# Attention masks of a two-layer decoder kernel: masks kept in their own pool, one identity tile read with stride zero, and a first attention masked by GpSimd

## The chip, the cores and the metric

The kernel runs on one core of a Trainium2 chip. The metric is the device time of one launch in microseconds, from the first to the last instruction and what lies around them, as the median over several runs. TensorE does the matmuls (PE in the profile; PEld is its weight load), VectorE is DVE, ScalarE is ACT, GpSimd is POOL, and SyncE (SP) issues most of the transfers.

## The reference

Two layers run over 1024 prompt tokens and 32 sample tokens (8 sequences of 4). What matters here is layer 0:

- one projection gives the queries, keys and values of four attentions and a gate;
- attention A (g = 0 in the code) has 8 query heads on 2 key heads of size 64, a window of 128 keys back, and a learned sink in the denominator;
- attention B has three groups (g = 1, 2, 3) with windows and strides (128, 1), (512, 4), (2048, 16), 8 query heads on 2 key heads each, merged by their denominators;
- the sample tokens do the same attention against long caches of keys and values;
- then gate, output projection, residual and LayerNorm.

```
dist = query - key;  band = (dist >= 0) & (dist <= span)     # blocks of 128: own block and the one before
p = exp(where(band, q.k, -1e30) - max);  out = p @ v / sum(p)
x1 = LayerNorm(alpha * x + (mix * silu(z)) @ w_out)
```

Layer 1 (an mLSTM) comes after it and is not touched.

## The kernel before

The program is written as one stream of operations over tiles. The framework (`schedule_with_timeline_sim=True`) fixes each engine's order when the kernel is built: it walks a model of time and gives each engine, among the operations that are ready by the model, the one with the best priority. On the chip each engine and each queue of transfers keeps that order, so an operation that waits holds up all that stands behind it. Tiles come from pools that are laid out in SBUF as a stack; a new pool may cover the bytes of one that was released, and what is written there first waits for the last use of what lay there before.

Layer 0 goes in four steps.

1. `proj_kv` and `proj_q(0)` project the keys, the values and A's queries.
2. `projections()` (queries of B, in chunks `pj` of 384, 384 and 288 tokens, L199 to L201) is woven with `attention()`: A whole (`attn_a` for two key heads) and the row maxima of B's first two groups (`stats`, tile `st`).
3. `gate_path()` is woven with `attention_b()`: the last maxima, then `attn_b(0)` and the first nine blocks of `attn_b(1)`.
4. The pool `sm` is released (L967). The rest of `attn_b(1)` (`late`), the sample tokens' attention (`sample_attn`) and the first `merges` are woven. The sample attention loads its keys and values (inputs `in_kt`, `in_vc`) into tiles `KT` of a new pool `smt` with four buffers, 24 loads in all; their lines are L672 (scores `sS`) and L719 (outputs `so`). Then `out0` follows: the weights `in_wo` go through `wr` into `oh` and `ol`, `out_proj` multiplies them with the merged `M` into `py` (L165 to L167, 24 matmuls for each half of a block of 128 tokens, two PSUM banks for each half), and adds the residual `xr` (L870), which lies in a pool `lnp` opened above the weights.

`scores` makes a block of attention: for 128 queries of four heads and 128 keys it fills a PSUM tile `sc` with three matmuls of 512 columns, the first of which adds the mask: the weights are a 128x128 tile of `maskr`, the moving operand is four identities side by side, `ident4` (the trace writes it `ident`). Two Exp on ScalarE give `ph` (rounded) and `p`, VectorE or at times GpSimd takes `pl` = `p` - `ph`, and three matmuls of 512 columns add `ph` and `pl` times `V` to `av`. A has 15 blocks for each key head, 30 in all; B has 70. `maskr` and `ident4` lie in `sm`, at its start, followed by `sinkb`, `sinkc`, the two query tiles `QZ` and then the small ones (`ST`, `junk`, `NM`, `dn`, `nmc`). The last use of a small one is `finish(1, 0)` with `dn`, at the end of `attn_b(0)`.

GpSimd also makes the low part `wl` of each projection weight (L122) and a sum in the rotation (L215). ScalarE also takes `pj` out of PSUM (L112).

Of the kernel before, what the change touches and what calls it, by code (L numbers as in the profile page):

```python
# [4 lines left out]
F32 = mybir.dt.float32  # L5
F32R = mybir.dt.float32r
AF = mybir.ActivationFunctionType
# [46 lines left out]
def run(g):  # L54
    for _ in g:
        pass
# [41 lines left out]
class Builder:  # L98
# [351 lines left out]
    def scores(self, g, kv, hf, Q1, Q2, K1, K2, V, emit):  # L450
        nc = self.nc
        for qb in range(2 * hf, 2 * hf + 2):
            q0 = 128 * (qb % 2)
            bl = self.blocks(g, qb)
            sct, avt = self.bps
            av = self.pp.tile([66, 512], F32, tag=avt[qb % len(avt)], name="av")
            for bi, (kb, kind) in enumerate(bl):
                sc = self.pp.tile([128, 512], F32, tag=sct[self.nsc % len(sct)], name="sc")
                self.nsc += 1
                ks = slice(128 * kb, 128 * kb + 128)  # L460
                so = sc.rearrange("p (h q) -> p h q", h=4)
                mk = self.maskr[:, 256:384] if g == 3 else self.maskr[:, 128 - 128 * kind:256 - 128 * kind]
                nc.tensor.matmul(so, mk, self.ident4, start=True, stop=False)
                nc.tensor.matmul(so, K1[:, ks], Q1[:, :, q0:q0 + 128], start=False, stop=False)
                nc.tensor.matmul(so, K2[:, ks], Q2[:, :, q0:q0 + 128], start=False, stop=True)  # L465
                ph = self.ppool.tile([128, 512], F32R, tag="ph", name="ph")
                pl = self.ppool.tile([128, 512], F32R, tag="pl", name="pl")
                p = self.ppool.tile([128, 512], F32, tag="p", name="p", bufs=3)
                nc.scalar.activation(ph, sc, AF.Exp)  # L469
                nc.scalar.activation(p, sc, AF.Exp)  # L470
                if g and self.nsc % POOL_LO == 0:
                    nc.gpsimd.tensor_tensor(pl, p, f(ph), OP.subtract)
                else:
                    self.lo(pl, p, ph)
                first, last = bi == 0, bi == len(bl) - 1
                nc.tensor.matmul(av, V[:, kb, 64:130], ph, start=first, stop=False)
                nc.tensor.matmul(av[0:64], V[:, kb, 0:64], ph, start=False, stop=False, skip_group_check=True)
                nc.tensor.matmul(av, V[:, kb, 64:130], pl, start=False, stop=last)
            emit(qb, av)
            yield 1.1 * len(bl)  # L480
# [395 lines left out]
    def layer0(self):  # L876
        nc, tc, A, O = self.nc, self.tc, self.A, self.O
        dp = self.dram
        dt = lambda n, s: dp.tile(s, F32, name=n)

        self.QQ = [dt(f"QQ{g}", [129 * 8, TP]) for g in range(4)]
        self.QS = dt("QS", [4, 512, TS])

        self.KK, self.KS = dt("KK", [2 * 512, TP]), dt("KSd", [512, TS])

        self.VV = dt("VV", [TP, 8 * 128])
        self.NMB = [[dt(f"NMB{i}{g}", [4, TP]) for g in range(3)] for i in range(2)]

        self.OD = [[dt(f"OD{t}{i}", [65, 4, TP]) for i in range(2)] for t in range(2)]
        self.FD = [[dt(f"FD{t}{i}", [4, TP]) for i in range(2)] for t in range(2)]  # L890
        self.SZ = dt("SZ", [8, 128, T])
        self.KVN = dt("KVN", [TS, 2, 512])
        self.X1 = dt("X1", [T, 1024])

        self.X0 = [(self.xp.tile([128, 8, n], F32R, tag=f"xh{c}", name=f"xh{c}"),
                    self.xp.tile([128, 8, n], F32R, tag=f"xl{c}", name=f"xl{c}")) for c, (t0, n) in enumerate(CH)]
        self.wsp = tc.alloc_tile_pool(name="wsp", bufs=2, side="right")
        stage = self.stage = tc.alloc_tile_pool(name="stage", bufs=2, side="right")
        tmp = self.tmp = tc.alloc_tile_pool(name="tmp", bufs=1, side="right")
        self.proj_kv()  # L900
        with tc.tile_pool(name="qp", bufs=2) as self.qp, tc.tile_pool(name="kp", bufs=2) as self.kp, \
                tc.tile_pool(name="vp", bufs=2) as self.vp, tc.tile_pool(name="ppool", bufs=3) as self.ppool, \
                tc.tile_pool(name="odp", bufs=1) as self.odp:
            sm = self.sm = tc.alloc_tile_pool(name="sm", bufs=1)

            raw = self.wraw.tile([128, 1024], F32, tag="wraw", name="mkr")
            self.load(raw[:, 0:384], A['maskq'])
            self.maskr = self.sm.tile([128, 384], F32R, name="maskr")
            self.hi(self.maskr, raw[:, 0:384])
            self.maskq = f(self.maskr)  # L910
            self.ident4 = self.sm.tile([128, 4, 128], F32R, name="ident4")
            nc.vector.tensor_copy(self.ident4, self.ident.unsqueeze(1).to_broadcast([128, 4, 128]))
            self.sinkb = self.sm.tile([128, 64], F32, name="sinkb")
            self.load(self.sinkb, A['sinkb'])
            self.sinkc = self.sm.tile([32, 2], F32, name="sinkc")
            self.load(self.sinkc, A['sinkc'])
            self.QZ = [sm.tile([128, 4, 256], F32R, name=f"QZ{u}") for u in range(2)]
            for Q in self.QZ:
                nc.gpsimd.memset(f(Q[64:128]), 0.0)
            run(self.proj_q(0))  # L920
            self.done = 0
            self.bps = AB_PS[0]

            def projections():
                for g in (1, 2, 3):
                    yield from self.proj_q(g)
                    self.done = g

            def attention():
                for kv in range(2):  # L930
                    yield from self.attn_a(kv)
                for g in (1, 2):
                    while self.done < g:
                        yield None
                    for kv in range(2):
                        yield from self.attn_b_stats(g, kv)

            weave((projections(), W1[0]), (ahead(tc, attention(), AHEAD[0]), W1[1]))

            tmp.release()  # L940
            tmp = self.tmp = tc.alloc_tile_pool(name="tmpz", bufs=1, side="right")

            def gate_path():
                for j in range(8):
                    yield from self.proj_z0(j)

            def last(c):
                if c < 2:
                    self.merge0(1, 1, c, self.M, False)

            def attention_b():
                for kv in range(2):
                    yield from self.attn_b_stats(3, kv)
                    self.attn_b_max(kv)
                self.bps = AB_PS[1]
                yield from self.attn_b(0)
                late = self.late = self.attn_b(1, last)
                for _ in range(EARLY):
                    yield next(late)

            weave((gate_path(), W2[0]), (ahead(tc, attention_b(), AHEAD[1]), W2[1]))
            tmp.release()
            stage.release()
            self.wsp.release()
            self.x2p = tc.alloc_tile_pool(name="x2p", bufs=1, side="right")
            self.mp = tc.alloc_tile_pool(name="mp", bufs=1, side="right")
            sm.release()  # L967
            M = self.M = [(self.xp.tile([128, 8, n], F32R, tag=f"xh{c}", name=f"mh{c}"),
                           self.xp.tile([128, 8, n], F32R, tag=f"xl{c}", name=f"ml{c}"))
                          for c, (t0, n) in enumerate(CH)]  # L970

            def merges(cs):
                for c in cs:
                    for ty, kv in ((0, 0), (0, 1), (1, 0)):
                        self.merge0(ty, kv, c, M)
                        yield 1.0

            self.bps = AB_PS[2]
            with tc.tile_pool(name="smt", bufs=4) as st:
                sp = Scratch(*(self.x2p.tile([128, 3072], F32, tag=f"x{u}x2", name=f"scr{u}") for u in "hl"))  # L980
                weave((ahead(tc, self.late, AHEAD[2]), W3[0]), (ahead(tc, self.sample_attn(sp, st), AHEAD[2]), W3[1]),
                      (merges((0, 1)), W3[2]))
            self.merge0(1, 1, 2, M, False)
            run(merges((2,)))

    def out0(self):
        nc, tc, A = self.nc, self.tc, self.A
# [628 lines left out]
```

## Time and profile before

| | us |
|---|---|
| median of 3 runs (1510.17 to 1512.73) | 1512.56 |
| the profiled execution | 1509.37 |
| its span, first to last instruction | 1507.6 |
| TensorE busy | 1419.9 |
| VectorE busy | 891.0 |
| ScalarE busy | 511.7 |
| GpSimd busy | 180.5 |
| mean granted TensorE clock, share of full | 0.974 |

Busy times are sums over instructions. A busy TensorE isn't one at its peak, since ends of matmuls are modelled and overlap; what a matmul costs is read from start to start. The granted clock is a share of 2.4 GHz; 0.5 is the lower level, 1.2 GHz.

### The profile page before, as it was taken

Reading aid. Unit: us, or ns where it says so; the run is one execution under the profiler, and the core shown is the slowest. Engines: PE = TensorE matmul, PEld = TensorE weight load, DVE = VectorE, ACT = ScalarE, POOL = GpSimd, SP = SyncE. Lnnn points to the kernel's source line nnn. Section 1 sums busy time; section 2 is a strip of 40 time slices with the busy share of each in tenths; the row PEclk is TensorE's granted clock in tenths of the full one; section 3 lists DMA queues with packets and bytes.
Section 4 is the critical chain, followed back from the end, with each engine's and each line's share of the span. In section 5 each row is a group of like instructions: output and inputs, shape, how many; then the busy total and the mean of one; then the engine's idle time right before and its main releaser. Section 6 shows DMA issues by size and latency. Waiting matters only on the chain.

```text
span 1507.6 us, 22066 instructions
## 1 busy us (share of the span) xinstructions
PE 1419.9 (94%) x7892; PEld 1205.5 (80%) x7892; DVE 891.0 (59%) x2480; ACT 511.7 (34%) x939; POOL 180.5 (12%) x219
## 2 busy tenths in 40 slices
PE   8999999999998889688999999999999999999997
PEld 8989999998897555446879878988898899877885
DVE  5311455557676867666674535555665566566786
ACT  5332244442223777321114313331333133323310
POOL 1002221212220222100000000000000000000010
PEclk9999999999999899798999999999999999999999
DMA  8446655447753664794212565364223323341741
GB/s 295 168 142 196 200 169 179 155 151 203 204 172 123 195 181 136 215 296 167 88 54 77 200 218 182 94 220 133 73 73 125 116 57 68 113 133 23 241 138 46
DMA packets 139307, 226.86 MB, mean 150 GB/s; under 512 B 17216, under 2 KB 107296, under 8 KB 138680
## 3 DMA queue, kind: packets, MB, share of 16 engines
q1 hardware_dynamic: 131134, 204.09, 44.0%
q10 hardware_dynamic: 8064, 21.37, 4.1%
q8 instruction: 63, 1.03, 0.3%
q14 instruction: 46, 0.38, 0.1%
HBM read 166.60 MB, written 81.88 MB: 165 GB/s over the span
## 4 chain that ended last, share of the span: by engine, by line
PE 68%; DMA 17%; DVE 7%; issue 3%; ACT 2%; SPq 1%; POOL 1%; DVEq 0%; POOLq 0%; ACTq 0%
PE pj L199 10%; PE pj L201 10%; PE pj L200 10%; PE py L167 3%; PE py L165 3%; PE py L166 3%; PE pvo L165 3%; PE pvo L166 3%; PE pvo L167 3%; DMA G<-GR 3%; DMA wr<-in_wo_dram 2%; DMA QZ<-QQ 1%; DMA OD<-OD 1%; DMA out_cmems_dram<-Cs 1%; DMA Q<-QQ 1%
## 5 line engine op out<-in xcount | busy, mean ns | idle before, releaser
L199 PE MATMUL pj<-xh,wh 128*128 128x384 f32 (+1 forms) x576 | 186.4, 324 | 5.9 <-DVE sl L117 3.1
L199 PE MATMUL pj<-x1h,wh 128*128 128x384 f32 (+1 forms) x576 | 189.7, 329 | 1.7 <-ACT QT L1149 1.6
L201 PE MATMUL pj<-x1h,wl 128*128 128x384 f32 (+1 forms) x576 | 187.8, 326 | 0.0
L200 PE MATMUL pj<-x1l,wh 128*128 128x384 f32 (+1 forms) x576 | 187.6, 326 | 0.0
L201 PE MATMUL pj<-xh,wl 128*128 128x384 f32 (+1 forms) x576 | 185.6, 322 | 0.0
L200 PE MATMUL pj<-xl,wh 128*128 128x384 f32 (+1 forms) x576 | 185.4, 322 | 0.0
L199 PEld LDWEIGHTS pj<-xh,wh 128*128 128x128 f32 x576 | 108.2, 188 | 10.0 <-DVE sl L117 4.0
L199 PEld LDWEIGHTS pj<-x1h,wh 128*128 128x128 f32 x576 | 108.7, 189 | 6.5 <-issue 3.3
L201 PEld LDWEIGHTS pj<-x1h,wl 128*128 128x128 f32 x576 | 108.6, 188 | 6.0 <-issue 5.8
L200 PEld LDWEIGHTS pj<-x1l,wh 128*128 128x128 f32 x576 | 108.6, 189 | 4.0 <-issue 3.8
L201 PEld LDWEIGHTS pj<-xh,wl 128*128 128x128 f32 x576 | 108.2, 188 | 1.2
L200 PEld LDWEIGHTS pj<-xl,wh 128*128 128x128 f32 x576 | 108.2, 188 | 1.2
L437 DVE CUSTOM_DVE_ANT_0 junk<-st,maskr 128x256 f32<-128x256 f32 (+1 forms) x256 | 93.1, 364 | 23.6 <-PE st L433 9.8
L165 PE MATMUL pvo<-voh,x1h 128*128 128x512 f32 x256 | 101.2, 398 | 2.8 <-DVE SZ L1165 2.8
L166 PE MATMUL pvo<-voh,x1l 128*128 128x512 f32 x256 | 100.3, 395 | 0.0
L167 PE MATMUL pvo<-vol,x1h 128*128 128x512 f32 x256 | 99.6, 392 | 0.0
L798 POOL TENSOR_TENSOR rsw<-rsw,mhalf 128x1 f32<-128x1 f32 (+1 forms) x54 | 39.9, 738 | 329.1 <-DVE rsw L797 313.5
L122 POOL TENSOR_TENSOR wl<-wr,wh 128x1024 fp32r<-128x1024 f32 x24 | 57.8, 2410 | 174.7 <-ACT qs L233 127.7
L112 ACT ACTIVATE wh<-wr 128x1024 fp32r<-128x1024 f32 x48 | 50.7, 1057 | 71.3 <-PE pj L200 63.1
L469 ACT ACTIVATE ph<-sc 128x512 fp32r<-128x512 f32 x100 | 59.2, 593 | 38.9 <-PE sc L465 24.2
L116 DVE TENSOR_TENSOR pl<-p,ph 128x512 fp32r<-128x512 f32 x82 | 59.2, 733 | 20.9 <-ACT p L470 20.8
L165 PE MATMUL py<-oh,mh 128*128 128x512 f32 x128 | 53.3, 416 | 12.3 <-ACT oh L112 9.0
(349 smaller groups left out, 3153.3 us busy)
## 6 DMA issues: line engine op xcount, KB each, us to landing
Q<-QQ SPq DMA_DIRECT2D x32, 512.0 KB
out_kvs_dram<-in_cache_b_kv_dram SPq DMA_DIRECT2D x16, 1022.0 KB
wr<-in_w0f_dram SPq DMA_DIRECT2D x24, 512.0 KB
wr<-in_w1f_dram SPq DMA_DIRECT2D x24, 512.0 KB
QQ<-sh ACTq DMA_DIRECT2D x16, 512.0 KB
QQ<-sl ACTq DMA_DIRECT2D x16, 512.0 KB
QZ<-QQ SPq DMA_DIRECT2D x32, 256.0 KB
wr<-in_wo_dram SPq DMA_DIRECT2D x16, 512.0 KB
```

Of the source, the lines that this page charges most:

```text
L112: return self.nc.scalar.activation(out, in_, AF.Copy, scale=scale)
L116: return self.nc.vector.tensor_tensor(out, in_, f(hi), OP.subtract)
L122: self.nc.gpsimd.tensor_tensor(out, in_, f(hi), OP.subtract)
L165: nc.tensor.matmul(ps, xh[:, k, t], wh, start=k == 0, stop=False)
L166: nc.tensor.matmul(ps, xl[:, k, t], wh, start=False, stop=False)
L167: nc.tensor.matmul(ps, xh[:, k, t], wl, start=False, stop=k == 7)
L199: nc.tensor.matmul(ps[:, :n], wh[:, k, :], xh[:, k, :n], start=k == 0, stop=False)
L200: nc.tensor.matmul(ps[:, :n], wh[:, k, :], xl[:, k, :n], start=False, stop=False)
L201: nc.tensor.matmul(ps[:, :n], wl[:, k, :], xh[:, k, :n], start=False, stop=k == 7)
L437: nc.vector.tensor_tensor_reduce(junk[:, :n], st[:, u, c0:c0 + n], mk, 1.0, -3e38, OP.add, OP.max, ST[:, 8 * h + qb:8 * h + qb + 1])
L469: nc.scalar.activation(ph, sc, AF.Exp)
L798: nc.gpsimd.tensor_tensor(r, v, self.mhalf[:m], OP.pow)
```

## The change

The two mask tiles move from `sm` to a pool `mk` that is opened below `sm` and released after the last merge. The four identities become one, `identr`, that the mask matmul reads four times with stride zero. For A the mask matmul is left out: the unmasked scores go through one Exp into `p`, GpSimd's `affine_select` sets the masked elements of `p` to zero, and ScalarE copies `p` into `ph` (`self.hi`). For B the order of the two Exp stays; `p` is allocated ahead of `pl`.

```diff
@@ scores
-                nc.tensor.matmul(so, mk, self.ident4, start=True, stop=False)
-                nc.tensor.matmul(so, K1[:, ks], Q1[:, :, q0:q0 + 128], start=False, stop=False)
+                if g:
+                    mk = ...
+                    nc.tensor.matmul(so, mk, self.identr.unsqueeze(1).to_broadcast([128, 4, 128]), start=True, stop=False)
+                nc.tensor.matmul(so, K1[:, ks], Q1[:, :, q0:q0 + 128], start=not g, stop=False)
                 nc.tensor.matmul(so, K2[:, ks], Q2[:, :, q0:q0 + 128], start=False, stop=True)
+                p = self.ppool.tile([128, 512], F32, tag="p", name="p", bufs=3)
                 ph = self.ppool.tile([128, 512], F32R, tag="ph", name="ph")
+                if g:
+                    nc.scalar.activation(ph, sc, AF.Exp)
+                    nc.scalar.activation(p, sc, AF.Exp)
+                else:
+                    nc.scalar.activation(p, sc, AF.Exp)
+                    nc.gpsimd.affine_select(p, p, [[0, 4], [-1 if kind else 1, 128]], OP.is_ge, 0.0, base=0,
+                                            channel_multiplier=1 if kind else -1)
+                    self.hi(ph, p)
                 pl = self.ppool.tile([128, 512], F32R, tag="pl", name="pl")
-                p = self.ppool.tile([128, 512], F32, tag="p", name="p", bufs=3)
-                nc.scalar.activation(ph, sc, AF.Exp)
-                nc.scalar.activation(p, sc, AF.Exp)
@@ layer0
+            mk = tc.alloc_tile_pool(name="mk", bufs=1)
             sm = self.sm = tc.alloc_tile_pool(name="sm", bufs=1)
-            self.maskr = self.sm.tile([128, 384], F32R, name="maskr")
+            self.maskr = mk.tile([128, 384], F32R, name="maskr")
-            self.ident4 = self.sm.tile([128, 4, 128], F32R, name="ident4")
-            nc.vector.tensor_copy(self.ident4, self.ident.unsqueeze(1).to_broadcast([128, 4, 128]))
+            self.identr = mk.tile([128, 128], F32R, name="identr")
+            nc.vector.tensor_copy(self.identr, self.ident)
...
             run(merges((2,)))
+            mk.release()
```

## Rows read from the trace of the kernel before

**Rows 1.** Busy times of the page: engine, us, share of the span, instructions.
```profile
PE 1419.9 (94%) x7892; PEld 1205.5 (80%) x7892; DVE 891.0 (59%) x2480; ACT 511.7 (34%) x939; POOL 180.5 (12%) x219
```

**Rows 2.** Stretches: length, PE, PEld, DVE, ACT, POOL busy, granted clock, DMA, GB/s.
```profile
190.00:260.00 70.00, 70.00 (x404) 63.58 (x402) 39.12 (x93) 33.79 (x57) 15.48 (x9) 1.00 0.53 165
260.00:345.00 85.00, 82.76 (x483) 75.69 (x482) 46.72 (x119) 36.23 (x60) 16.45 (x9) 1.00 0.49 157
...
560.00:606.60 46.60, 42.46 (x178) 26.08 (x176) 32.36 (x48) 37.17 (x65) 12.39 (x9) 1.00 0.44 131
606.60:617.20 10.60, 4.88 (x24) 1.82 (x24) 10.29 (x12) 1.09 (x2) 2.67 (x1) 0.71 0.60 185
...
606.60:690.70 84.10, 58.22 (x364) 34.01 (x364) 50.37 (x86) 21.14 (x44) 5.77 (x3) 0.79 0.82 255
690.70:800.00 109.30, 107.41 (x533) 88.44 (x534) 80.20 (x167) 20.02 (x34) 8.80 (x10) 0.97 0.25 85
```

**Rows 3.** SP's queue: issue start, issue us, transfer, how many.
```profile
559.11 0.33 SPq L109 DMA_DIRECT2D FD<-dn  x1
...
605.70 1.65 SPq L106 DMA_DIRECT2D KT<-in_kt_dram  x2
...
620.50 0.85 SPq L109 DMA_DIRECT2D OD<-OD  x1
...
686.46 1.28 SPq L106 DMA_DIRECT2D xr<-in_xtok_dram  x3
```

**Rows 4.** Waits of SP's queue, 603 to 606 and then 678 to 687 us.
```profile
SPq L106 <- PE sc L463: 2.9, 1, 2.9
...
SPq L106 <- PE so L719: 2.0, 1, 2.0
```

**Rows 5.** TensorE in order of time: start, us, operation [idle before it].
```profile
211.95 0.40 PE L463 MATMUL sc<-ident,maskr 128*128 128x512 f32 x1
212.18 0.39 PE L464 MATMUL sc<-Q,K 128*128 128x512 f32 x1
...
567.98 1.06 PE L641 MATMUL sNew<-scrh,scrl 128*128 128x32 f32 x8
...
605.23 0.44 PE L463 MATMUL sc<-ident,maskr 128*128 128x512 f32 x1
...
626.16 0.80 PE L165 MATMUL py<-oh,mh 128*128 128x512 f32 x1 [9.01 <-ACT oh L112]
...
664.12 1.07 PE L167 MATMUL py<-ol,mh 128*128 128x512 f32 x4
...
684.48 1.91 PE L719 MATMUL so<-KT,scrh 128*32 128x128 f32 x32
...
690.74 0.80 PE L165 MATMUL py<-oh,mh 128*128 128x512 f32 x1 [3.27 <-DVE xr L870]
```

**Rows 6.** Groups of instructions, 190 to 345 us: busy us, mean ns, idle before.
```profile
L122 POOL TENSOR_TENSOR wl<-wr,wh 128x1024 fp32r<-128x1024 f32 x9 | 21.6, 2401 | 95.3 <-ACT qs L233 91.6 <-ACT wh L112 3.7
...
L463 PE MATMUL sc<-ident,maskr 128*128 128x512 f32 x30 | 11.8, 393 | 0.0
```

**Rows 7.** Line L472 on GpSimd: ns min/median/max, first and last start.
```profile
L472 POOL TENSOR_TENSOR pl<-p,ph x18: 1262/1293/2927, 477.6 to 613.7; 128x512 fp32r<-128x512 f32 x18
```

**Rows 8.** TensorE groups, 560 to 690.7 us.
```profile
L167 PE MATMUL py<-ol,mh 128*128 128x512 f32 x32 | 10.2, 420 | 0.0
...
L672 PE MATMUL sS<-KT,scrl 128*32 128x512 f32 x32 | 8.0, 603 | 1.6 <-DMA KT<-in_kt_dram 0.8 <-PE sS L672 0.8
```

**Rows 9.** Transfers, 560 to 690.7 us, and three links of the chain that ended last.
```profile
DMA packets 15700, 27.57 MB, mean 211 GB/s; under 512 B 1267, under 2 KB 10926, under 8 KB 15690
...
540.49 4.57 DMA Q<-QQ
...
638.62 6.58 DMA wr<-in_wo_dram
645.26 7.94 DMA KT<-in_kt_dram
```

More of the change, by code (lines that the diff above doesn't have):

```diff
@@ L461, in scores @@
                 so = sc.rearrange("p (h q) -> p h q", h=4)
-                mk = self.maskr[:, 256:384] if g == 3 else self.maskr[:, 128 - 128 * kind:256 - 128 * kind]
-                nc.tensor.matmul(so, mk, self.ident4, start=True, stop=False)
-                nc.tensor.matmul(so, K1[:, ks], Q1[:, :, q0:q0 + 128], start=False, stop=False)
+                if g:
+                    mk = self.maskr[:, 256:384] if g == 3 else self.maskr[:, 128 - 128 * kind:256 - 128 * kind]
+                    nc.tensor.matmul(so, mk, self.identr.unsqueeze(1).to_broadcast([128, 4, 128]), start=True, stop=False)
+                nc.tensor.matmul(so, K1[:, ks], Q1[:, :, q0:q0 + 128], start=not g, stop=False)
                 nc.tensor.matmul(so, K2[:, ks], Q2[:, :, q0:q0 + 128], start=False, stop=True)
+                p = self.ppool.tile([128, 512], F32, tag="p", name="p", bufs=3)
                 ph = self.ppool.tile([128, 512], F32R, tag="ph", name="ph")
+                if g:
[6 more added lines that the diff above has]
+                    self.hi(ph, p)
                 pl = self.ppool.tile([128, 512], F32R, tag="pl", name="pl")
-                p = self.ppool.tile([128, 512], F32, tag="p", name="p", bufs=3)
-                nc.scalar.activation(ph, sc, AF.Exp)
-                nc.scalar.activation(p, sc, AF.Exp)
                 if g and self.nsc % POOL_LO == 0:
```

## Prediction

> **What bounds the kernel now.** I read the page's busy times first, then TensorE's idle time by stretches, then the order of TensorE and of SP's queue where TensorE is idle. TensorE is the engine to watch: it is busy 94% of the span, the next engine 59% [rows 1]. While attention A runs, from 190 to 345 us, it is idle for only 2.24 us of 155 at full clock [rows 2]: there, a matmul less is time saved, as long as its replacement keeps up. The stretch with room is 606.6 to 690.7 us: 58.22 us busy of 84.1, and a granted clock of 0.79, so part of the busy time ran at 1.2 GHz [rows 2].
>
> The order shows why. The sample attention's first scores of the new tokens, which need no `KT`, are done by 569 us [rows 5], but the first two `KT` loads are issued at 605.70 [rows 3]. SP's queue had waited 2.9 us for L463, the mask matmul [rows 4], and the last L463 is at 605.23 [rows 5]. So `KT` lay on the bytes of the mask tiles, and the sample attention, all of its 24 loads, came after the last masked block of B. Its last matmul, L719, starts at 684.48 and runs 1.91 us to 686.39 [rows 5]; at 686.46 the three loads of the residual `xr` go out [rows 3], released by that L719 [rows 4]. The output projection had meanwhile filled its four PSUM banks with two blocks of 128 tokens, up to about 665, and could go on only once `xr` was added: at 690.74, after VectorE's L870 [rows 5]. Two waits in a row, mask tile to `KT` and `KT` to `xr`, hold the output projection back.
>
> **The change part by part.**
>
> *A's mask matmul.* 30 instructions go [rows 6]. From start to start one costs 212.18 - 211.95 = 0.23 us [rows 5]; 30 x 0.23 = 7 us of a TensorE that has no idle time to lose. The Trainium skill (TensorE: Matmul & The Clock Gate, "Wait — 56ns, not 53.3ns?") gives N / 2.4 GHz + 2.5 ns from start to start at the full clock; for 512 columns this is an estimate of 0.216 us, and the saving by it would be 6.5 us. The row is for these very operands, so 7 stands.
>
> *A's GpSimd mask.* Before, `ph` needs one Exp; now it needs Exp, `affine_select` and a copy. ScalarE still has two instructions a block and VectorE one. No `affine_select` is in the trace. The nearest row is GpSimd's `pl` on the same 128x512, median 1.293 us, longest 2.927 [rows 7]; I take 1.3. From below, an operation with no cost at all adds nothing; from above 2.9. GpSimd gets 30 x 1.3 = 39 us on top of 15.48 + 16.45 = 31.9 us in 155 [rows 2], which fits. What hides the longer chain is the projection: with `pj` matmuls planned between scores and `av`, TensorE goes on while a block waits. If that cover were gone, 1.3 us a block would be 39 us. Two queues feel it: on GpSimd a mask can stand behind a `wl` of 2.4 us [rows 6], and `wl` behind masks; on ScalarE the copy that waits for GpSimd holds up the emptying of `pj`, which has two banks. I charge 2 us in all (bounds 0 and 39). A: -7 + 2 = -5.
>
> *One identity with stride zero.* The mask matmuls of B still stream 512 columns. L464 already reads 128 columns out of a tile's 256 for each head and takes 0.39 us beside the 0.40 of L463 [rows 5], so pieces of 128 columns cost nothing there: I take 0. It is made once, ahead of A, from a quarter of the elements: 0 too.
>
> *The pool `mk`.* No operation is added; what changes is who waits. `smt` now covers only what is left of `sm`: `QZ`, `ST`, `junk` and `dn`. The last of these to be used is `dn`, whose store goes out at 559.11 [rows 3], some 2 us ahead of the next transfer on that queue. So `KT` may start at about 561 in place of 605.7, at most 44 us earlier. `xr` then waits for the late mask matmuls and for a sample attention that ends earlier; the late matmuls end by 606 anyway.
>
> How early can TensorE start its third token block (690.74 before)? Three limits:
>
> - *The shift itself.* If the sample attention only moves, its end goes from 686.4 to 686.4 - 44 = 642, `xr` follows, and the third block could start at 647, which is -44.
> - *TensorE's order.* The late blocks ended at 617 (626.16 less 9.01 of idle time, [rows 5]). The sample attention's matmuls now come among them: 96 `py` matmuls (three lines of 32 [rows 8]) at 0.23 are 22 us; the sample attention is the rest, some 16 us at full clock (8.0 of it busy time of L672 [rows 8], the others in small pieces; an estimate). Of 57 us from 560 to 617 TensorE was idle for 4.1 up to 606.6 and for 5.7 after it [rows 2], so the late blocks slip by 16 - 10 = 6 us at least, to about 624. The store of `OD` (620.50 [rows 3]) and the first weights follow, and the first `py`, at 626.16 [rows 5], comes at 633. Two token blocks end there at 633 + 22 = 655 if the weights keep up, and the third starts at 657: -34.
> - *The transfers.* 27.57 MB moved from 560 to 690.7 [rows 9], at 131 GB/s up to 606.6 and 255 after [rows 2]. Some 2.5 MB (`xr`, layer 1's first weight) may come later; 25 MB at the 255 of that stretch from 561 on take 98 us, to 659, -32; at 310, which I take as reachable since the stretch holds idle parts, 81 us, to 642.
>
> I take -32. After the wait TensorE began at its lower clock: the mean of 0.97 over 109.3 us [rows 2] is 3.3 us of work not done. A TensorE that hasn't waited gets most of it back, 2.5 us. Against it, `Q` loads of the late blocks (4.57 us in the chain) will share the engines with `KT` (7.94 us in the crowd) [rows 9]: I charge 4 us for longer waits there. So -32 - 2.5 + 4 = -30.5; bounds 0 (nothing gained) and 44 + 3 = -47. Where the stall goes: the output projection runs on until it wants the last merges, which need the sample attention's output; they are first read by the seventh token block, six blocks of 48 x 0.23 = 11 us on, so they don't decide. From there on TensorE is busy 107.41 of 109.3 [rows 2] and carries the gain to the end.
>
> *Sum.* 1509.4 (profiled) - 5 - 30.5 = 1474. The median of the runs shown lies 3.2 above the profiled execution; I forecast the median 1477.
>
> **The rivals.**
>
> *`KT` doesn't come earlier.* Something else that `smt` covers, or a place late in SP's order, keeps the first load near 600. For it: the order is a plan, and L463's wait took only 2.9 us of SP's time [rows 4]. Against it: that wait was planned for, and the load went out 0.03 us after the mask's last read at 605.67 [rows 3, 5]. Then only A's 5 us remain: 1507 in the median.
>
> *The gain is shared away.* `KT` starts early, but 10 MB of it among the late blocks delay `Q`, merges and weights; the late blocks end at 635 rather than 624, and half the gain is left: 1477 + 16 = 1493. For it: weights and `KT` took 6.58 and 7.94 us a load when crowded [rows 9]. Against it: the DMA share was 0.44 from 560 to 606.6 [rows 2].
>
> *A gets slower than all this gains.* TensorE waits for GpSimd in every block of A: the plan's price for `affine_select` is too low, `av` stands first in TensorE's order and nothing passes it. At 2.9 us [rows 7] and no cover, 30 x 2.9 - 7 = 80 us lost, and 1509.4 - 30.5 + 80 = 1559, 1562 in the median. It decides from (7 + 30.5) / 30 = 1.25 us of TensorE's waiting per block on. For it: GpSimd's operations stretch to 2.9. Against it: of 152.8 us of TensorE's work in that stretch [rows 2] A's own matmuls are 30 x 6 x 0.23 = 41, and the rest can run meanwhile. The Trainium skill (GPSIMD Engine Reference, "4.1 Engine selection") speaks against the move too: it sends elementwise work on a tile to VectorE, not GpSimd; no run here shows this operation on either.
>
> **How the numbers follow.** 0.2% (3 us) is about what a measurement tells from no change here. Forecast, 1462 to 1491: 0.57. Gain shared away, 1491 to 1503: 0.16. `KT` not earlier, 1503 to 1509: 0.11. Slower by A's waits: 0.09. These and A's waits eating the gain: same 0.05; even better than 1462: 0.02. The range takes the first two and most of the third: 1462 to 1507. Faster: 0.57 + 0.16 + 0.11 + 0.02 = 0.86; same 0.05; slower 0.09.
>
> **What would show it.** In the profile after: no L463 before the B stage and 30 `affine_select` on GpSimd near 1.3 us; TensorE idle in A's stretch by no more than some 4 us; the first `KT` load near 555 to 565, with B's masks still running; the last L719 before 650; the wait of L870 for `xr` gone, and the granted clock near 1 from 630 on. I am wrong if `KT` starts late, if ScalarE's copy shows long waits for GpSimd with TensorE behind it, or if the late blocks' end slips past 640.

## Result, and the profile after

| | before | after |
|---|---|---|
| median of 13 runs each, us | 1512.37 (1507.0 to 1514.8) | 1503.45 (1495.3 to 1508.3) |
| ratio after / before | | 0.9943, 95% interval 0.9925 to 0.9961 |
| span of the profiled execution, us | 1507.6 | 1501.7 |

The kernel is faster, by 0.6%, and inside the range (1462 to 1507). But the forecast was 1477, a gain of 35 us, and 9 were measured. Most of what the prediction said of single steps can be found in the trace; the gain is missing mainly in one place.

First the page's line of busy times, then stretches with the columns of [rows 2]:

```profile
PE 1413.6 (94%) x7862; PEld 1205.3 (80%) x7862; DVE 897.2 (60%) x2480; ACT 512.1 (34%) x939; POOL 204.8 (14%) x249
```

```profile
190.00:260.00 70.00, 70.00 (x413) 64.62 (x412) 43.42 (x108) 34.45 (x57) 26.43 (x24) 1.00 0.55 167
260.00:345.00 85.00, 80.07 (x458) 74.21 (x457) 54.06 (x142) 38.65 (x62) 28.94 (x24) 0.96 0.55 173
560.00:606.60 46.60, 41.09 (x211) 22.99 (x212) 33.44 (x65) 28.97 (x57) 8.35 (x7) 0.93 0.76 233
606.60:690.70 84.10, 62.58 (x349) 42.63 (x346) 53.79 (x77) 28.51 (x52) 6.09 (x5) 0.86 0.71 206
690.70:800.00 109.30, 107.45 (x563) 90.00 (x562) 81.40 (x168) 22.76 (x38) 8.06 (x9) 1.00 0.25 85
```

Beside [rows 2], the DMA share from 560 to 606.6 has gone from 0.44 to 0.76: the sample keys now move under the late blocks. But from 606.6 to 690.7 TensorE is busy for 62.6 us where it had been for 58.2, at a granted clock of 0.86 instead of 0.79. That stretch was to lose most of its idle time, and it still has 21.5 us of it.

SP's queue, beside [rows 3]:

```profile
555.26 0.57 SPq L109 DMA_DIRECT2D FD<-dn  x1
559.67 0.84 SPq L106 DMA_DIRECT2D KT<-in_kt_dram  x2
...
638.66 0.33 SPq L106 DMA_DIRECT2D wr<-in_wo_dram  x1
643.16 0.33 SPq L106 DMA_DIRECT2D xr<-in_xtok_dram  x1
643.58 0.38 SPq L106 DMA_DIRECT2D wr<-in_wo_dram  x1
...
653.64 2.63 SPq L106 DMA_DIRECT2D wr<-in_wo_dram  x2
...
663.76 6.11 SPq L106 DMA_DIRECT2D wr<-in_wo_dram  x2
```

TensorE, beside [rows 5] (the matmul that was L719 is L726 here, the residual's L870 is L877):

```profile
633.09 0.50 PE L165 MATMUL py<-oh,mh 128*128 128x512 f32 x1 [1.26 <-ACT oh L112]
...
641.20 1.92 PE L726 MATMUL so<-KT,scrh 128*32 128x128 f32 x28 [2.05 <-DMA KT<-in_vc_dram]
...
674.26 0.50 PE L165 MATMUL py<-oh,mh 128*128 128x512 f32 x1 [0.75 <-ACT oh L112]
...
682.45 0.80 PE L165 MATMUL py<-oh,mh 128*128 128x512 f32 x1 [5.13 <-DVE xr L877]
```

`KT` begins at 559.67 (before: 605.70), the sample attention ends at 643 (686), `xr` follows it, and the first `py` comes at 633.09. But the third token block begins at 682.45, where 657 was forecast. Two blocks of `py`, 22 us of work, took from 633 to 677. What they waited for stands on ScalarE, which splits the weights `wr` into `oh` and `ol`:

```profile
631.98 2.00 ACT L112 ACTIVATE oh<-wr 128x1024 fp32r<-128x1024 f32 x2 [0.37 <-DMA OD<-OD]
...
648.55 1.06 ACT L112 ACTIVATE oh<-wr 128x1024 fp32r<-128x1024 f32 x1 [3.44 <-DMA wr<-in_wo_dram]
...
661.42 1.06 ACT L112 ACTIVATE oh<-wr 128x1024 fp32r<-128x1024 f32 x1 [0.79 <-DMA wr<-in_wo_dram]
...
673.15 1.06 ACT L112 ACTIVATE oh<-wr 128x1024 fp32r<-128x1024 f32 x1 [0.45 <-DMA wr<-in_wo_dram]
```

After the first two the weights are loaded two at a time, at 638.66 and 643.58, from 653.64 and from 663.76, and the last is split at 673.15. Each block of `py` sums over all eight, so the second ends at 677.3. The third waits 5.13 us more for VectorE's L877. Ahead of that stand the last merges, with waits of their own, in VectorE's order:

```profile
678.52 0.23 DVE L840 TENSOR_TENSOR mz<-mz,scrh 128x64 f32<-128x64 f32 x1 [3.05 <-DMA mz<-SZ]
680.79 0.22 DVE L840 TENSOR_TENSOR mz<-mz,scrh 128x64 f32<-128x64 f32 x1 [2.04 <-DMA mz<-SZ]
...
681.71 1.28 DVE L877 SCALAR_TENSOR_TENSOR xr<-xr,py 128x512 f32<-128x512 f32 x2
```

The trace of before had such pairs of weights too; its last split, on ScalarE:

```profile
660.06 1.06 ACT L112 ACTIVATE oh<-wr 128x1024 fp32r<-128x1024 f32 x1 [1.94 <-DMA wr<-in_wo_dram]
```

There it was hidden, since the third block waited for `xr` until 690.74 anyway.

A's part, as instructions of line L474 on GpSimd (ns: shortest, median, longest), and then TensorE's only row of waits from 190 to 345 us:

```profile
L474 POOL TENSOR_SCALAR_AFFINE_SELECT p<-p x30: 629/706/1757, 203.1 to 311.6; 128x512 f32<-128x512 f32 x30
```

```profile
PE st L433 <- DMA QZ<-QQ: 4.9, 2, 2.9
```

`affine_select` takes 0.706 us in the median, about half of what was assumed, and TensorE doesn't wait for it. It waits for the `QZ` loads of the maxima, 4.9 us in all.

### The profile page after: what moved, and what is told of

It reads as the page before. It is cut to its first block, busy times and chain, and to the rows that moved or that the text cites. A ratio compares the mean times of both kernels' runs of the same rounds, so it can differ in the third digit from the quotient of the medians.

```text
span 1501.7 us, 22028 instructions
## 1 busy us (share of the span) xinstructions
PE 1413.6 (94%) x7862; PEld 1205.3 (80%) x7862; DVE 897.2 (60%) x2480; ACT 512.1 (34%) x939; POOL 204.8 (14%) x249
## 4 chain that ended last, share of the span: by engine, by line
PE 70%; DMA 16%; DVE 8%; issue 3%; ACT 2%; SPq 1%; POOL 0%; DVEq 0%; ACTq 0%; POOLq 0%
PE pj L199 10%; PE pj L201 10%; PE pj L200 10%; PE py L165 3%; PE py L167 3%; PE py L166 3%; PE pvo L165 3%; PE pvo L166 3%; PE pvo L167 3%; DMA Q<-QQ 3%; DMA QZ<-QQ 2%; DMA G<-GR 2%; PE st L433 1%; DMA mo<-OD 1%; DMA out_cmems_dram<-Cs 1%
## 5 line engine op out<-in xcount | busy, mean ns | idle before, releaser
L116 DVE TENSOR_TENSOR pl<-p,ph 128x512 fp32r<-128x512 f32 x82 | 63.1, 776 | 26.8 <-ACT p L471 15.2
L122 POOL TENSOR_TENSOR wl<-wr,wh 128x1024 fp32r<-128x1024 f32 x24 | 58.2, 2427 | 129.7 <-ACT qs L233 57.8
L433 PE MATMUL st<-K,QZ 128*128 128x256 f32 x256 | 52.5, 294 | 11.6 <-DMA QZ<-QQ 7.3
```

Source lines behind the costliest of these rows:

```text
L116: return self.nc.vector.tensor_tensor(out, in_, f(hi), OP.subtract)
L122: self.nc.gpsimd.tensor_tensor(out, in_, f(hi), OP.subtract)
L433: nc.tensor.matmul(st[:, u, :], Q1[:, h, q0:q0 + 128], K1[:, w0:w0 + 256], start=True, stop=True)
```

## Experiments

All times are ratios to the kernel before, run on the same chip in the same rounds. Two landmarks are used throughout: the split of the last weight on ScalarE, and the first addition of a residual `xr` on VectorE, behind which the third token block starts. From that addition to the end of the span all of these kernels take 815 to 822 us; what is decided is decided ahead of it. The framework plans the order of the operations anew for each run, so a run differs from its neighbour by its edit and by an order of its own; what a mere order is worth is measured under "What A's part does".

### The parts by themselves

The first run takes A's part and the one identity, with the tiles left in `sm`; the second the pool and the one identity, with A masked by matmul:

```diff
 # e2_pool_alone, against the change
-                if g:
+                if True:
                     mk = ...
                     nc.tensor.matmul(so, mk, self.identr..., start=True, stop=False)
...
-                if g:
+                if True:
                     nc.scalar.activation(ph, sc, AF.Exp)
                     nc.scalar.activation(p, sc, AF.Exp)
 # e1_masks_only, against the change
-            self.maskr = mk.tile([128, 384], F32R, name="maskr")
+            self.maskr = self.sm.tile([128, 384], F32R, name="maskr")
...
-            self.identr = mk.tile([128, 128], F32R, name="identr")
+            self.identr = self.sm.tile([128, 128], F32R, name="identr")
```

> A's part alone: A masked by GpSimd, one identity with stride zero, but both tiles stay in the pool that is released ahead of the sample attention. If the two parts of the change add up, this gives what the changed kernel had gained by 559 us (3.9 us in its trace): 1508 to 1509 beside 1512.4, ratio 0.997, with the first KT load still right behind the last mask matmul, near 601 us. Rival: GpSimd's longer chain costs as much as the 30 matmuls give, and the whole gain is the pool's: ratio 1.000.

> The pool alone: mask tiles in the pool that lives on (with the one identity, since four of them leave too little room), A masked by matmul as before. If the parts add up: first KT load near 563, TensorE's third token block of the output projection near 686 in place of 690.7, ratio 0.996 to 0.998. If the whole gain were the pool's: ratio 0.994. If the pool alone gave what was forecast for it: ratio 0.98.

The third makes nothing but the identity one tile, read with stride zero; the fourth is the change with A not masked at all:

```diff
 # e3_stride_alone, against before
-                nc.tensor.matmul(so, mk, self.ident4, start=True, stop=False)
+                nc.tensor.matmul(so, mk, self.identr.unsqueeze(1).to_broadcast([128, 4, 128]), start=True, stop=False)
...
 # e4_a_unmasked, against the change
-                if g:
-                    nc.scalar.activation(ph, sc, AF.Exp)
-                    nc.scalar.activation(p, sc, AF.Exp)
-                else:
-                    nc.scalar.activation(p, sc, AF.Exp)
-                    nc.gpsimd.affine_select(p, p, ...)
-                    self.hi(ph, p)
+                nc.scalar.activation(ph, sc, AF.Exp)
+                nc.scalar.activation(p, sc, AF.Exp)
```

> Only the one identity read with stride zero, in the old pool. If a stride of zero costs nothing: mask matmuls of 0.39 us as before, ratio 1.000 within 0.002. If it costs, 100 mask matmuls are longer and the ratio is above 1.002. If a mere shift of tiles and of the planned order moves the time by as much as the change did, the ratio is off by some 0.005 either way.

> The changed kernel with A's mask left out altogether (no matmul, no GpSimd; two Exp as before), so A's output is another: what the GpSimd chain costs. If it is hidden: the same time as the changed kernel within 2 us, 1501 to 1505, ratio to before 0.993 to 0.995. If the chain makes TensorE wait: faster than the changed kernel by 4 us or more, ratio 0.991 or less.

| run | ratio | 95% interval | last maxima stored | first `KT` | last weight | first `xr` added |
|---|---|---|---|---|---|---|
| before | 1 | | 477.7 | 605.7 | 660.1 | 690.0 |
| the change | 0.9943 | 0.9925 to 0.9961 | 470.9 | 559.7 | 673.2 | 681.7 |
| e1, A and identity | 1.0078 | 1.0055 to 1.0102 | 478.1 | 615.8 | 671.8 | 705.1 |
| e2, pool and identity | 0.9917 | 0.9898 to 0.9936 | 476.4 | 559.5 | 668.6 | 676.5 |
| e3, identity | 1.0008 | 0.9991 to 1.0024 | 477.8 | 608.7 | 664.9 | 696.9 |
| e4, A unmasked | 0.9971 | 0.9952 to 0.9991 | 479.9 | 564.1 | 677.8 | 686.9 |

The pool alone gives the whole gain, 0.83% or 12.5 us (its interval and the change's overlap); stride zero costs nothing that can be measured, as taken. A's part by itself makes the kernel slower, which neither theory had expected. And leaving A's mask out altogether, matmul and GpSimd both, isn't faster than the change (0.9971, above both of its expectations): no cost of GpSimd's 0.7 us a block is seen. Two questions follow: what stopped the pool's gain at 12.5 us, and what A's part does.

### What stops the pool's gain

Three suspects: the bytes that must pass ahead of the third block, the order on SP's queue (in the change the load at 643.58, of weight 3 counted from 0, stands behind an `xr` load), and the two buffers `wraw` through which the weights go. The runs start from e2.

```diff
 # g1_half_sample_keys
-        for u in range(2):
-            t = st.tile([128, 2, 4, 128], F32, tag="KT", name="KT")
-            s = 4 * a + 2 * u
-            self.load(t, src[:, s:s + 2])
-            out += [t[:, 0], t[:, 1]]
+        t = st.tile([128, 2, 4, 128], F32, tag="KT", name="KT")
+        self.load(t, src[:, 4 * a:4 * a + 2])
+        for u in range(2):
+            out += [t[:, 0], t[:, 1]]
 # g2_wo_other_queue, in load_wo
-        self.load(raw, src[:, k, :])
+        (self.nc.sync if self.layer else self.nc.gpsimd).dma_start(raw, src[:, k, :])
 # g3_xr_other_queue, in out_proj
-                    self.load(xr[:m], xres[128 * i:128 * i + m])
+                    (self.nc.sync if self.layer else self.nc.gpsimd).dma_start(xr[:m], xres[128 * i:128 * i + m])
```

> The pool and the one identity, with A masked by matmul as before, and half of the sample keys and values of types 2 and 3 left out: the first of each pair of KT loads serves for both, so that 8 loads of 0.52 MB (4.2 MB of the 28 MB that pass between 560 us and the third token block) are not made and the sample outputs differ. Without this cut the pool alone gave a ratio of 0.992 and its third block began at about 677. Theory 1, the transfers ahead of the third token block set its start: 4.2 MB at 230 to 310 GB/s are 13 to 18 us, so the third block at 659 to 664 and a ratio of 0.980 to 0.984. Theory 2, the order on SP's queue and the two staging buffers of the weights set it, whatever the bytes: third block at 673 or later, ratio 0.989 to 0.992.

> The pool and the one identity, A masked by matmul, and the eight loads of the output projection's weights of this layer issued by GpSimd instead of SP, so that they don't stand behind the xr loads and the merges. Theory 1 (bytes): the third block stays within 3 us of 677, ratio 0.990 to 0.993. Theory 2 (order on SP's queue): the weights k=2 to 7 come 5 to 10 us earlier, third block at 667 to 672, ratio 0.985 to 0.989. Against both: GpSimd's merges (mo by mf) would wait behind a weight load that waits for its buffer, and the time would be no better than 0.992.

> The pool and the one identity, A masked by matmul, and the loads of the residual rows xr of this layer issued by GpSimd instead of SP, so that no weight load stands behind an xr load. Theory 1 (bytes): 0.990 to 0.993, third block within 3 us of 677. Theory 2 (order on SP's queue): the weight loads behind xr come 3 to 5 us earlier and the third block with them, ratio 0.988 to 0.990.

| run | ratio | 95% interval | first `py` | last weight | first `xr` added |
|---|---|---|---|---|---|
| e2 | 0.9917 | 0.9898 to 0.9936 | 634.2 | 668.6 | 676.5 |
| g1, 4.2 MB less | 0.9898 | 0.9870 to 0.9927 | 638.5 | 669.7 | 675.1 |
| g2, weights on GpSimd's queue | 0.9909 | 0.9889 to 0.9930 | 627.8 | 669.2 | 676.1 |
| g3, `xr` on GpSimd's queue | 0.9907 | 0.9886 to 0.9928 | 634.2 | 670.4 | 678.1 |

None moves the third block by more than 2 us: a seventh of the bytes can go (23.75 MB pass from 560 to 677 us in g1, 27.96 in e2), and either load can leave SP's queue, and the last weight still comes at 669 to 670. Two things these runs don't reach. g1's missing bytes lie ahead of 644; from there to 656, where weights are under way, the DMA engines are as full in g1 as in e2 (a busy share of 1.06 in both). And e2 hasn't the order that was suspected in the change; its loads of weights 2 and 3 go out together, ahead of `xr`:

```profile
637.33 1.46 SPq L106 DMA_DIRECT2D wr<-in_wo_dram  x2
...
645.36 2.66 SPq L106 DMA_DIRECT2D xr<-in_xtok_dram  x3
```

In the change VectorE had freed both buffers by 639.61, and the second load went out 4 us later, behind `xr`:

```profile
637.26 2.35 DVE L116 TENSOR_TENSOR ol<-wr,oh 128x1024 fp32r<-128x1024 f32 x2
```

So the order on SP's queue delays that load by some 4 us in the change, which none of these three runs tests; it doesn't explain what holds e2. g2 shows what does. With the weights on GpSimd's queue, the wait of each issue stands in that engine's rows (start, issue time, idle time before it and who ended it):

```profile
632.63 0.59 POOL L846 DMA_DIRECT2D wr<-in_wo_dram  x1 [15.15 <-DVE ol L116]
633.77 0.53 POOL L846 DMA_DIRECT2D wr<-in_wo_dram  x1 [0.55 <-DVE ol L116]
643.32 0.53 POOL L846 DMA_DIRECT2D wr<-in_wo_dram  x1 [9.03 <-DVE ol L116]
644.89 0.53 POOL L846 DMA_DIRECT2D wr<-in_wo_dram  x1 [1.04 <-DVE ol L116]
...
658.11 0.59 POOL L846 DMA_DIRECT2D wr<-in_wo_dram  x1 [2.43 <-DVE ol L116]
665.01 0.53 POOL L846 DMA_DIRECT2D wr<-in_wo_dram  x1 [6.31 <-DVE mz L840]
```

Five of the six wait for `ol`, the second half of the split of the weight that held their buffer. One trip is: issue, landing, `oh` on ScalarE, `ol` on VectorE. Six weights through two buffers are three trips, in a row, and the first can't start before the late blocks have freed the space for `oh` and `ol` (first split at 627 to 637 in these runs). In g2 that split was 6 us earlier than in e2, and the last still came at 669.15: the trips were longer (on VectorE a merge that waited 9.92 us for `mz` stood ahead of the `ol` of the third).

The next runs give the weights five more buffers, from a pool in space that becomes free there, in e2 and, as a control, in the kernel before:

```diff
-            W = [self.load_wo(A['wo0'], k, *self.wo_tiles(wp, k)) for k in range(8)]
             with tc.tile_pool(name="lnc", bufs=1) as lc:
+                ws = tc.alloc_tile_pool(name="ws", bufs=5)
+                W = [self.load_wo(A['wo0'], k, *self.wo_tiles(wp, k), ws if k in (2, 3, 4, 5, 6) else None) for k in range(8)]
+                ws.release()
...
     def load_wo(self, src, k, h, l, pool=None):
+        if pool:
+            raw = pool.tile([128, 1024], F32, tag="wx", name="wr")
+        else:
+            raw = self.wraw.tile([128, 1024], F32, tag="wraw", name="wr")
```

> The pool and the one identity, A masked by matmul, and five more staging buffers for the output projection's weights of this layer (a pool of their own in the space that becomes free at about 633; k=2 to 6 land there, k=0, 1 and 7 in the two buffers of before). Without them the weights came in rounds of two, each some 11 us (loads at 637, 649 and 660, last conversion at 668.6), and the third token block began at about 677. Theory S, the rounds through two buffers set the third block: the loads k=2 to 6 go out together at 633 to 638, the last conversion is at 655 to 660, the third block at 660 to 667, ratio 0.981 to 0.986. Theory 1 (bytes) and a rival, DVE's merges and reciprocals in front of the conversions: the last conversion stays at 665 or later, the third block within 4 us of 677, ratio 0.989 to 0.993.

> The kernel before with the same five staging buffers for the weights and nothing else. There the weights were through at 660 and the third block began at 690.7, behind the residual rows whose loads went out at 686.5, behind the KT loads. Theory S: nothing to gain, since the weights aren't last here, ratio 0.998 to 1.002, third block at 687 to 693. Rival, the buffers help by themselves, whatever the pool: 0.990 or lower.

i1: 0.9861 (0.9838 to 0.9885), 1488.3 us. SP's queue, ScalarE and VectorE of i1, one fence each (L877 is L880 here):

```profile
636.04 0.33 SPq L106 DMA_DIRECT2D wr<-in_wo_dram  x1
...
643.77 4.08 SPq L106 DMA_DIRECT2D wr<-in_wo_dram  x5
```

```profile
652.66 3.08 ACT L112 ACTIVATE oh<-wr 128x1024 fp32r<-128x1024 f32 x3
656.64 1.06 ACT L112 ACTIVATE oh<-wr 128x1024 fp32r<-128x1024 f32 x1 [0.90 <-DMA wr<-in_wo_dram]
```

```profile
665.31 0.69 DVE L880 SCALAR_TENSOR_TENSOR xr<-xr,py 128x512 f32<-128x512 f32 x1 [0.16 <-PE py L167]
```

Five loads go out in one row, the last weight is split at 656.6 (668.6 in e2), and the first residual is added at 665.3 (676.5), right behind TensorE's last `py`. 11 us at the landmark became 0.0056 of the time, 8.5 us. Not all of the 11 are the weights'. In e2 the last `py` of the two blocks ended at 672.70, and the first addition stood behind two merges that waited for `mz`, until 676.51; in the order of i1 it stands ahead of them. So 7.5 us are the weights' and 3.7 that order's. The weights' part doesn't hang on an order: from the first split to the last it takes 32 to 43 us in all fourteen kernels with two buffers, and 24.5 and 27.6 us in i1 and j3 (below), though the DMA engines are as full there (a busy share of 1.06 and 1.04 from 638 to 656, 1.04 in e2). The trips through two buffers were the limit.

i2: 1.0080 (1.0064 to 1.0096). It was expected to be neutral, and is slower. TensorE and then SP's queue of i2:

```profile
680.64 1.92 PE L719 MATMUL so<-KT,scrh 128*32 128x128 f32 x28 [0.52 <-DMA KT<-in_vc_dram]
```

```profile
682.61 2.29 SPq L106 DMA_DIRECT2D wr<-in_wo_dram  x5
```

The last matmul that reads `KT` ends at 682.56, and the five loads go out at 682.61, after SP's queue had waited 1.9 us for it. The new pool lies on `KT`'s bytes, as `KT` had lain on the mask tiles': with the late `KT` of before, buffers that were meant to bring the weights earlier made them later. The residual is added at 700.2 (690.0). So the buffers don't help by themselves; they help once the sample attention comes early.

### What A's part does

```diff
 # g4_both_masks_in_A, against the change: A's matmul put back, GpSimd kept
-                if g:
+                if True:
                     mk = ...
 # i3_weave_73, i4_weave_79, against e2; j1_change_weave_73, j2_change_weave_79, against the change
-W1, W2, W3, W4 = (129, 76), (86, 80), (28, 15, 6), (64, 90)
+W1, W2, W3, W4 = (129, 73), (86, 80), (28, 15, 6), (64, 90)    # 79 in i4 and j2
 # j3_change_five_weight_buffers: the diff of i1, against the change
```

> The whole change with A's mask matmul put back, so that A is masked twice, by the matmul and by GpSimd: TensorE's work in A is that of before, the chain Exp, affine_select, copy is that of the change. Theory A1, what A's part costs is the chain through GpSimd and the second pass of ScalarE: the cost stays and the 30 matmuls of 0.22 us come on top, ratio 0.994 + 0.004 = 0.998 or more. Theory A2, it comes from leaving the matmuls out (TensorE runs dry, waits for the loads of Q, and the orders behind it are planned anew): with the matmuls back the ratio is that of the pool alone, 0.990 to 0.993.

> The pool and the one identity, A masked by matmul, and the weight of the attention in the first weave set from 76 to 73, so that the same operations are written in a slightly different order: no work is added or removed. Without this the ratio is 0.992. Theory P, what A's part costs is what any new order of stage 3 costs or gives (the planner's orders scatter by 0.3 to 1%): one of this and the next run at least lies outside 0.989 to 0.994, and the differences arise between 200 and 560 us. Theory C, the order is worth little and GpSimd's chain is what costs: both inside 0.989 to 0.994.

> As the run before, with the weight set to 79. Theory P: one of the two at least outside 0.989 to 0.994. Theory C: both inside.

> The whole change with the weight of the attention in the first weave at 73 instead of 76. A by matmul with the pool gave 0.9917 at 76, 1.0028 at 73 and 1.0029 at 79; A by GpSimd with the pool gave 0.9943 at 76. Theory C, A by GpSimd costs by itself: 0.002 to 0.005 above the run with the matmul at each weight, so 1.005 to 1.008 here. Theory P, the order decides and A by GpSimd is worth little or a gain: no such steady difference; at one weight at least A by GpSimd is faster, 1.001 or less.

> The whole change with the weight at 79. Theory C: 1.005 to 1.008. Theory P: 1.001 or less here or in the run before.

> The whole change with the five more staging buffers for the weights. With A by matmul they took the pool from 0.9917 to 0.9861 and the first result of the third block's row from 676.5 to 665.3. Theory S, the rounds through two buffers hold the whole change too: last conversion at 660 or earlier (673.2 without), ratio 0.986 to 0.990. If not: 0.992 to 0.996, last conversion after 668.

All of these have the pool. Side by side:

| order | A by matmul | A by GpSimd |
|---|---|---|
| weight 76 | e2: 0.9917 (0.9898 to 0.9936) | the change: 0.9943 (0.9925 to 0.9961) |
| weight 73 | i3: 1.0028 (1.0015 to 1.0041) | j1: 0.9940 (0.9919 to 0.9962) |
| weight 79 | i4: 1.0029 (1.0013 to 1.0046) | j2: 0.9950 (0.9931 to 0.9968) |
| 76, five buffers | i1: 0.9861 (0.9838 to 0.9885) | j3: 0.9865 (0.9842 to 0.9888) |

g4, with both masks, has 0.9948 (0.9928 to 0.9967). It met neither expectation: the time is that of the change, so 30 matmuls more show no cost beside what a new order may bring.

The theory that GpSimd's chain costs by itself falls with j1 and j2: at two of three orders A by GpSimd is 0.8 to 0.9% *faster* than A by matmul. i3 and i4 do the same work as e2 and are 1.1% slower; a change of the writing order in step 2 alone is worth more than all of A's part. In i3, where TensorE waited longest from 260 to 410 us, and then, on SP's queue, the store of B's last maxima and of its first denominators `FD`:

```profile
PE st L433 <- DMA QZ<-QQ: 8.1, 3, 4.3
```

```profile
494.76 0.94 SPq L109 DMA_DIRECT2D NMB<-NM  x1
...
578.97 0.33 SPq L109 DMA_DIRECT2D FD<-dn  x1
```

And the same two stores in j1:

```profile
471.20 0.33 SPq L109 DMA_DIRECT2D NMB<-NM  x1
...
556.64 0.33 SPq L109 DMA_DIRECT2D FD<-dn  x1
```

In e2 the maxima are stored at 476.39 and `FD` at 557.98. So i3 is 18 us late at the maxima and 21 at `FD`, and its longer waits for `QZ` are only 3.3 us of that (8.1 beside 4.8 in e2).

What follows `FD` keeps the pool's gain in every order. From that store to the first `xr` added it takes 131, 143, 134 and 141 us in the kernels without the pool (before, e1, e3, i2), 116 to 126.5 in the eleven with it and two buffers, i3 and i4 among them (119 and 122), and 107 and 109 in i1 and j3. The pool and the buffers shorten that stretch whatever the order; what i3 and i4 lose, they lose ahead of it.

The output of A's second half is stored at 322 to 326 us in the five kernels with GpSimd alone, and at 328 to 333 in the ten with the matmul alone. So A does become some 4 to 10 us shorter, in every order. Whether that is still there at 555 goes with the order in which the planner put the maxima of B (`st`, fed by the `QZ` loads) and the gates behind it: at 471 the change is 5.5 us ahead of e2, at 555 it is 2.7 ahead, at the first `py` 1.1, and at the last weight 4.6 behind. The last turn fits the 4 us of the load behind `xr`, an order that j1 and j2 have too (3.0 and 3.5 us) and e2, i3 and i4 haven't. In j3, where the weights don't hold it up, it ends level with i1.

## Why the prediction was right and wrong

**Right: the chain from mask tile to `KT` to `xr`.** `KT` was to start at about 561 and did at 559.67; the sample attention was to end before 650 and did at 643; the late blocks were to slip by an estimated 6 to 7 us and the first `py` to come at 633, and it came at 633.09. The rival that `KT` doesn't come earlier is out.

**Wrong: "Two token blocks end there at 633 + 22 = 655 if the weights keep up, and the third starts at 657".** The condition got no price. The weights don't keep up: 673 for the last one, and the third block at 682.45. That is 25 us late, nearly the whole miss of 26 (1503.45 against 1477): the two blocks end at 677.3 in place of 655, which is 22 us by the weights, and the other 3 are VectorE's merges, which wait for `mz` ahead of the first addition. The price of the weights was to be had from the trace of before: last split at 660.06 with the first at 625.05, three trips of two in 35 us. With the first split at 632, as the slip forecast, the last comes at 667, and with the 9 us that e2 and the change take from that split to the third block, it starts at 676: a gain of 15 us rather than 34, close to e2's 12.5 us. Three limits were set against each other, and the one that became the bound wasn't among them, since in the profile of before something longer hid it. That the time lies inside the range is owed to the rivals that the range takes in, not to the sum.

**Wrong: the limit by transfers, -32.** It came out beside the wrong -34 and looked like support. g1 leaves out 4.2 MB and gains 0.0019 of the time, within the intervals. The sum of the bytes wasn't the limit; what the full engines add to each trip of a weight wasn't measured apart.

**Two smaller terms.** The -2.5 for the clock came in part at most: TensorE had waited once more, and from 682.45 to 687.3 its matmuls follow each other every 0.43 us, after it every 0.23. The +4 for longer waits of the late blocks isn't seen, since the first `py` came where it was forecast without them. Three of the signs that were named failed: TensorE is idle for 4.93 us in A's stretch rather than some 4, the wait for the first addition is still there (5.13 us, now for the merges), and the granted clock is 0.86 from 606.6 to 690.7 rather than near 1.

**In part: "the gain is shared away".** Its time, 1493, was nearer than the forecast, and crowded weights were named in it. But it put the loss on the late blocks' end, at 635, and their last store of `OD` went out at 627.97.

**A's part: right in place, not in the sum.** -7 + 2 = -5 is near what A's end shows (329.7 to 323.1). +2 for GpSimd's chain was too high, if anything: 0.706 us instead of 1.3, no row of TensorE waiting for it, and ScalarE waiting for it for 1.0 us in all. The rival that A gets slower by waiting for GpSimd is out. The rule cited from the Trainium skill (GPSIMD Engine Reference, "4.1 Engine selection") isn't tested, since no run has the mask on VectorE; its row is on add, mul and max, and it calls GpSimd slower for two inputs, where `affine_select` has one. No run shows GpSimd's own time to cost: e4 without it isn't faster, j1 and j2 with it are. What failed is the step from A's end to the kernel's end, "a matmul less is time saved": TensorE's idle time in the stretch rose from 2.24 to 4.93 us, the clock granted from 260 to 345 fell from 1.00 to 0.96, and the new order behind it took the rest of the lead. A's part alone, e1, is 0.78% slower; on top of the pool +0.0026, -0.0088, -0.0079 and +0.0004, by the order.

**Right: stride zero at nothing.** e3: 1.0008 (0.9991 to 1.0024).

**Not settled.** Why 73 and 79 make bad orders with the matmul and not with GpSimd wasn't traced to one instruction, and the kernel before wasn't run at these weights, so what the pool is worth there in the whole time isn't known. Where e1 loses what it gains in A isn't settled either: it stores A's output 3.7 us before the kernel before, `FD` 2.7 us after it, and its first `KT` load, still behind the last mask matmul, is 10.1 us late. A run that holds the order of the other stages fixed while A changes wasn't made.

The best version is i1, 0.9861: the pool, one identity, five buffers for the weights; j3, with A by GpSimd, is level with it.

## What to carry to other kernels

When a wait is taken away, price the next thing that the released engine reads, even where it lies hidden now: here the trace of before had the split of the last weight at 660.06, and that time, shifted with the first split, gives 667, where 673 was measured. An "if it keeps up" in a sum is a term, with rows of its own. In a kernel whose order a planner writes, compare a local change at two or three orders before giving it a sign: the same operations, woven 76 or 73, differed by 1.1%, four times as much as A's part at 76.

## What the runs showed of the hardware

- `affine_select` in place on 128x512 took 0.706 us on GpSimd, while its subtraction of two such tiles took 1.29 [rows 7].
- The issue of a weight's load held GpSimd for 0.53 to 0.59 us (the rows of g2), an issue by SP its queue for 0.33 and more [rows 3].
- A second, unneeded mask by matmul (30 of 0.23 us, g4 against the change) and a seventh fewer bytes ahead of the third block (g1) changed nothing measurable. With two weights under way at a time, six took three trips and 32 to 43 us from the first split to the last; with five more buffers 24.5 and 27.6 us (i1, j3), through DMA engines as full.
